# Layer 0's first two modulation vectors from column-tiled float32 matmuls, with their weights in the tiles that later hold h

## The chip, the core and the metric

The kernel runs on one core of a Trainium2 chip. The metric is the device time of one execution in microseconds; a smaller time is better. All numbers ahead of the prediction belong to the kernel before the change.

## What is computed

Two layers of an encoder run over two groups of 512 tokens (g = 0 and 1) with 1024 features. Both groups share all weights; each has its own conditioning vector c. Cut to what matters here:

```python
for l in range(DEPTH):                                     # 2 layers
    mod = (jax.nn.silu(c) @ w_ada[l] + b_ada[l]).reshape(Bsz, 6, 1, D)
    shift_a, scale_a, gate_a = mod[:, 0], mod[:, 1], mod[:, 2]
    shift_f, scale_f, gate_f = mod[:, 3], mod[:, 4], mod[:, 5]
    h = rms_norm(x, norm_attn_g[l]) * (1.0 + scale_a) + shift_a
    proj = h @ w_in[l]
    ...                                                    # four kinds of attention heads
    x = x + gate_a * (mixed @ w_out[l])
    h = rms_norm(x, norm_ffn_g[l]) * (1.0 + scale_f) + shift_f
    x = x + gate_f * conv_glu_ffn(h, ...)
```

Everything is float32. The modulation vectors are numbered c6 = 0 to 5 in the order of the reshape, so c6 = 0 and 1 (shift and scale of the attention norm) are needed before the first h exists, and c6 = 2 to 4 of layer 0 only after the attention.

## The kernel before, in words

Layout: features lie on the 128 partitions in KC = 8 chunks, tokens along the free axis. Large products are made from three matmuls each (`mm3`, lines 172 to 174): both operands are split into a high part (`hh`, `whi`) and a rest (`hl`, `wlo`).

Start of the program (lines 321 to 453, pools `pa`, `pw`, `px`): c is loaded and silu'd into `csx` (line 333). `ada` (line 178) makes a modulation vector from `w_ada`. For c6 = 0 and 1 it is called with `whole=True`, first half (512 columns) of both vectors and then the second half of both: the weights come in pieces of 384 KB on SP's queue (line 191) into seven stage tiles `s` (four of `pw`, three of `pa`), and each piece is multiplied in plain float32, 256 columns at a time, with a stationary operand of 128 x 2 (line 198); 128 such matmuls in all. After each half DVE copies the row out (`arow`, line 205), four small transposes put it on the partitions (line 208), DVE adds the bias (line 216) and, for c6 = 1, makes the gain `ab` (line 225). Between the pieces the hook `interleave` places the eight loads of x (512 KB each, line 354) at the piece numbers `XPOS`. Then come four loads of the first unit's weights (`wt0`, line 379, through `W` of pool `wp`: two stage tiles, a ring of five `whi`/`wlo` pairs; the rest is subtracted by POOL). x is squared and summed (lines 264 to 268), the norm's row is built (lines 274 to 282), and lines 390 to 402 make the 16 pairs `hh`, `hl` from x, the modulation and the norm, mostly on DVE. The pairs live in pool `hp`, 16 tiles of 2 KB for each name.

The last thing in that block (line 453) is `ada(WA, pa, 0, c6, p_tp, p_ov)` for c6 = 2 to 4: 33 more pieces of 384 KB, queued on SP behind the `wt0` loads, each split into `whi` and `wlo` (line 160 on ACT, line 162 on DVE or POOL in the order v, v, p), with three stage tiles and three pairs in `pa`, and `arow` (2 KB, one tile) and `at4` (64 bytes, one tile) for each half vector's end. Its matmuls use the banks `p_tp` and `p_ov`. This is called "the stream" below.

Then the layer loop: nine units (C0, D0, C2, A0, ...) for both g give 18 steps. `project` (line 510) of a step makes four blocks of 128 tokens, 24 matmuls of 384 columns each; ACT copies each block out of its bank to `raw` (line 533) and `V` (line 536). Step 0 (C0, g = 0) uses the banks `p_mm`, `p_mm`, `p_sc`, `p_sc`; later steps of layer 0 use `p_mm` only. There are two banks of `p_mm` and two of `p_sc`. `prepare` (line 569) normalises and transposes `raw` (line 611) and stacks q and k by DMA (line 597). The scores follow (lines 676 and 677), with the bias loaded at line 484, then the softmax's minimum (line 641, writes `S` and `mn`).

Order: the plan at the end of `trunk_kernel` gives a program order, and the framework's list scheduler fixes the order of each engine's instructions when the program is built. Up to eight DMAs of SP's queue are under way at a time (eight semaphores, in turn). 

Memory: the pools lie one behind the other, each tag in the order of its first use, sizes rounded up to 32 bytes. `pa` holds `s` (3 x 3072 bytes per partition), `arow` (2048), `whi` and `wlo` (3 x 3072 each) and `at4` (64): 29,760 bytes. When `pa`, `pw` and `px` are closed, the attention's pools begin at `pa`'s first byte: `ap` (bias, `mx`, `mn`, `den`, `pth`, `ptl` and small tiles: 30,240 bytes), behind it `av` (two `raw` tiles of 4096, three `V` of 4096), then `ar` and `au`. With `reuse_waits="tile"` the first writer of a tile waits until every tile that lay on the same bytes before has been read for the last time. The first `bias` tile has offset 0, as `s`; the first `mn` has offset 9216, as `arow`; step 0's `raw` is the first tile of `av`.

Of the kernel before, what the change touches and what calls it, by code (L numbers as in the profile page):

```python
# [8 lines left out]
F32 = mybir.dt.float32  # L9
# [3 lines left out]
AF = mybir.ActivationFunctionType  # L13
ALU = mybir.AluOpType
# [11 lines left out]
EPS = 1e-6  # L26


P = {'w0': 2.41, 'w1': 2.07, 'b0': 1.49, 'j0': 1.86, 'j1': 1.0, 'p0': 1.06, 'p1': 0.83, 'v': 0.29, 'vd': 0.32, 'f': 0.13, 'fc': 1.16, 'm0': 2.02, 'm1': -0.42, 'o0': 0.58, 'o1': 0.68, 'o2': 0.44, 'a0': 0.66, 'a1': 3.46, 'S': 7, 'K': 6, 'R': 2, 'e': 'p', 'q': 'aa', 'r': 'pv', 'pd': 0.07, 's': -0.28, 'we': 'vvp', 'x': [4, 5, 6, 7, 13, 15, 17, 19], 'hl': 'vpvpvvvv', 'ul': 'v', 'us': 'p', 'ug': 'p', 'uc': 'v', 'uf': 'p', 'tb': 'vpv', 'tl': 'vvvp', 'ds': 'p', 'db': 'p', 'dl': 'vvp', 'd2': 'v', 'ft': [9, 10], 'td': [6, 8], 'fr': [4, 6], 'fs': 3, 'na': 6, 'n1': 2, 'n2': 2, 'gr': [[3, 3, 3], [4, 3, 4]], 'd0': 'v', 'd1': 'v', 't0': 4, 't1': 25, 'sa': [4, 2], 'at': [3.2, 21.2], 'ag': [[4, 4, 0], []]}
UNITS = ['C0', 'D0', 'C2', 'A0', 'D1', 'C1', 'B1', 'A1', 'B0']  # L30
CHUNK = {"A0": 0, "A1": 1, "B0": 2, "B1": 3, "C0": 4, "C1": 5, "C2": 6, "D0": 7, "D1": 8}
GSCALE = {"A": 64 ** -0.5, "B": 64 ** -0.5, "C": 64 ** -0.5, "D": 32 ** -0.5}
# [41 lines left out]
    pass  # L74


def trunk_kernel(tc, xT, cT, w_ada, w_adac, b_ada, norm_g, w_in, w_out, w_out2, w_out9, w_up, w_down, conv, qkn, rpb,
                 amask, t5, onehot, tmask, sink, lam_d, subln, blk, ident_in, out):
    nc = tc.nc
    with ExitStack() as ctx:  # L80
# [94 lines left out]

        ada_last = [None]

        def ada(W, pool, l, c6, bank=None, bank2=None, whole=False, hook=None, halves=(0, 1)):


            acc = None
            R = NG if whole else 2 * NG
            n = W.width // 256
            parts = [(b0, min(n, 16 * halves[-1] + 16 - b0)) for b0 in range(16 * halves[0], 16 * halves[-1] + 16, n)]
            for b0, nb in parts:
                src = w_ada[c6, :, b0 * 256:(b0 + nb) * 256]
                if not whole:
                    w = W.load(src, nb * 256)
                else:
                    w = (W.stage(),)  # L190
                    ada_last[0] = dma(w[0][:, :nb * 256], src).ins
                    hook(ada_last[0])
                for b in range(b0, b0 + nb):
                    half, q, k = b // 16, b // 8 % 2, b % 8
                    if b % 16 == 0:
                        acc = (bank or p_mm)()
                    for j, wj in enumerate(w):
                        nc.tensor.matmul(acc[:R, q * 256:(q + 1) * 256], cs[:, k] if whole else csr[:, k],
                                         wj[:, (b - b0) * 256:(b - b0 + 1) * 256],
                                         start=(k == 0 and j == 0 and q == 0),  # L200
                                         stop=(k == KC - 1 and j == len(w) - 1), skip_group_check=True)
                    if b % 16 < 15:
                        continue
                    row = pool.tile([128, 512], F32, name="arow", bufs=1)
                    nc.vector.tensor_copy(row[:R], acc[:R])
                    pt = (bank2 or p_pp)()
                    for d in range(4):
                        nc.tensor.transpose(pt[:, R * d:R * d + R], row[:R, d * 128:(d + 1) * 128], ident[:R, :R])
                    m = mod[:, l, c6, 4 * half:4 * half + 4]
                    t = pt[:, :4 * R].rearrange("p (a b) -> p a b", b=R)  # L210
                    if not whole:
                        t = pool.tile([128, 4, 4], F32, name="at4", tag="at4", bufs=1)
                        nc.vector.tensor_copy(t.rearrange("p a b -> p (a b)"), pt[:, :16])
                        nc.vector.tensor_tensor(m, t[:, :, 0:2], t[:, :, 2:4], op=ALU.add)
                        t = m
                    nc.vector.tensor_tensor(
                        m, t, bada[:, l, c6 * 8 + 4 * half:c6 * 8 + 4 * half + 4, None].to_broadcast([128, 4, 2]),
                        op=ALU.add)
            ada_gain(l, c6, halves)

        def ada_gain(l, c6, halves=(0, 1)):
            if c6 in (1, 4):
                j = c6 // 3
                a, b = 4 * halves[0], 4 * halves[-1] + 4
                nc.vector.scalar_tensor_tensor(
                    ab[:, l, j, a:b], mod[:, l, c6, a:b], 1.0,
                    ng[:, l, j, a:b, None].to_broadcast([128, b - a, 2]), op0=ALU.add, op1=ALU.mult)
# [93 lines left out]
        with tc.tile_pool(name="pa", bufs=1, reuse_waits="tile") as pa, \  # L321
# [32 lines left out]
                        dma(xs[g][:, k:k + 2], xT[:, g, k:k + 2])  # L354

            WA = Weights(pa, 768, 3, 3, tuple({'p': nc.gpsimd, 'v': nc.vector}[c] for c in P['we']))
            WS = Weights(px, 768, 0, 4)
            WX = Weights(pw, 768, 0, 4)
            stage_of = itertools.cycle((WX, WA, WX, WA, WX, WA, WX))
            WS.stage = lambda: next(stage_of).stage()  # L360
            for c6 in range(2):
                ada(WS, pa, 0, c6, whole=True, hook=interleave, halves=(0,))

            oh = pw.tile([32, 1280], F32, name="oh", bufs=1)
            t5_t = pw.tile([32, 14], F32, name="t5_t", bufs=1)
# [1069 lines left out]
def layout(i):  # L1435

    import numpy as np
    a = {k: np.asarray(v) for k, v in i.items()}
    chunks = lambda v: v.reshape(v.shape[:-1] + (-1, 128))
    r = {}  # L1440
    x = np.stack([a["x_prompt"][0], a["x_sample"][0]])
    r["xT"] = x.transpose(2, 0, 1).reshape(KC, 128, NG, T).transpose(1, 2, 0, 3)
    c = np.stack([a["c_prompt"][0], a["c_sample"][0]])
    r["cT"] = chunks(c).transpose(2, 1, 0)
    r["w_ada"] = a["w_ada"].reshape(DEPTH, KC, 128, 6, 4, 256).transpose(0, 3, 2, 4, 1, 5).reshape(DEPTH, 6, 128, 8192)[0, :5]
    w = a["w_ada"].reshape(DEPTH, KC, 128, 6, D)
# [12 lines left out]
    r["w_out2"] = w[:, others[6:]].transpose(0, 2, 3, 1, 4).reshape(DEPTH, 128, KC * 256)
# [25 lines left out]


# [20 lines left out]
```

## Time and profile before

| what | value |
| --- | --- |
| median of three runs | 2719.42 us (2717.59 to 2723.7) |
| the profiled execution, its own time | 2725.8 us |
| its span in the profile | 2724.0 us |
| TensorE (PE) busy | 2562.2 us, 94% of the span |
| VectorE (DVE) busy | 2018.2 us, 74% |
| ScalarE (ACT) busy | 1410.9 us, 52% |
| GpSimd (POOL) busy | 1143.0 us, 42% |
| granted TensorE clock, mean | 0.976 |

The profile shows one execution. A window row gives, for a stretch of time, each engine's busy time with its count of instructions, the granted TensorE clock, the share of the 16 DMA engines that was busy and the rate. A timeline row gives start, length, engine, line and tiles, with the idle time before it and what ended that. A DMA's row on SP is its issue, not its transfer.

### The profile page before, as it was taken

Reading aid. Unit: us, or ns where it says so; the run is one execution under the profiler, and the core shown is the slowest. Engines: PE = TensorE matmul, PEld = TensorE weight load, DVE = VectorE, ACT = ScalarE, POOL = GpSimd, SP = SyncE. Lnnn points to the kernel's source line nnn. Section 1 sums busy time; section 2 is a strip of 40 time slices with the busy share of each in tenths; the row PEclk is TensorE's granted clock in tenths of the full one; section 3 lists DMA queues with packets and bytes.
Section 4 is the critical chain, followed back from the end, with each engine's and each line's share of the span. In section 5 each row is a group of like instructions: output and inputs, shape, how many; then the busy total and the mean of one; then the engine's idle time right before and its main releaser. Section 6 shows DMA issues by size and latency. Waiting matters only on the chain. (4 is left out here: it accounts for less than half of the span.)

```text
span 2724.0 us, 39807 instructions
## 1 busy us (share of the span) xinstructions
PE 2562.2 (94%) x13836; PEld 2160.4 (79%) x13836; DVE 2018.2 (74%) x3639; ACT 1410.9 (52%) x3058; POOL 1143.0 (42%) x811
## 2 busy tenths in 40 slices
PE   8899999999879999998999999999996999999988
PEld 4788889888657777776788989898875888887767
DVE  6677577665887777789964765867469878878986
ACT  4466566564444445453444756756544555555422
POOL 2321212256644433428853122122667344441884
PEclk9999999999989999999999999999997999999999
DMA  7743545565144444452224345445651222224321
GB/s 265 217 116 107 130 109 141 145 188 181 66 163 144 142 140 128 151 205 101 93 76 113 86 114 136 113 118 148 191 181 47 86 78 87 76 86 185 109 85 62
DMA packets 146433, 347.69 MB, mean 128 GB/s; under 512 B 21372, under 2 KB 27260, under 8 KB 144952
## 3 DMA queue, kind: packets, MB, share of 16 engines
q1 hardware_dynamic: 133560, 322.08, 39.1%
q10 hardware_dynamic: 12672, 23.07, 2.3%
q8 instruction: 109, 1.79, 0.3%
q14 instruction: 92, 0.75, 0.1%
HBM read 241.19 MB, written 59.51 MB: 110 GB/s over the span
## 5 line engine op out<-in xcount | busy, mean ns | idle before, releaser
L162 POOL TENSOR_TENSOR wlo<-s,whi 128x768 fp32r<-128x768 f32 (+1 forms) x131 | 237.3, 1820 | 429.3 <-ACT whi L160 406.2
L172 PE MATMUL ps_mm<-hh,whi 128*128 128x512 f32 x932 | 369.7, 399 | 35.5 <-DVE t L1163 26.2
L173 PE MATMUL ps_mm<-hl,whi 128*128 128x512 f32 x932 | 369.0, 396 | 5.0 <-DVE hl L1094 3.7
L174 PE MATMUL ps_mm<-hh,wlo 128*128 128x512 f32 x932 | 367.5, 394 | 6.3 <-POOL wlo L1094 3.5
L172 PE MATMUL ps_mm<-whi,hh 128*128 128x256 f32 (+1 forms) x1104 | 342.0, 311 | 9.7 <-ACT raw L533 6.7
L173 PE MATMUL ps_mm<-wlo,hh 128*128 128x256 f32 (+1 forms) x1104 | 338.1, 307 | 1.3 <-POOL wlo L162 1.3
L174 PE MATMUL ps_mm<-whi,hl 128*128 128x256 f32 (+1 forms) x1104 | 337.9, 307 | 0.0
L1094 DVE TENSOR_TENSOR wlo<-fr,whi 128x512 fp32r<-128x512 f32 (+1 forms) x385 | 304.0, 807 | 38.2 <-ACT whi L1098 30.3
L1169 POOL TENSOR_TENSOR t<-t 128x512 f32<-128x512 f32 x88 | 127.9, 1453 | 428.0 <-issue 111.3
L1098 ACT ACTIVATE whi<-fr 128x512 fp32r<-128x512 f32 (+1 forms) x416 | 199.6, 517 | 176.3 <-PE ps_mm L173 65.5
L172 PEld LDWEIGHTS ps_mm<-hh,whi 128*128 128x128 f32 x932 | 176.2, 190 | 83.4 <-issue 22.0
L172 PEld LDWEIGHTS ps_mm<-whi,hh 128*128 128x128 f32 x1104 | 214.0, 194 | 13.4 <-ACT raw L533 7.5
L173 PEld LDWEIGHTS ps_mm<-wlo,hh 128*128 128x128 f32 x1104 | 214.3, 194 | 4.2 <-POOL wlo L162 2.2
L174 PEld LDWEIGHTS ps_mm<-whi,hl 128*128 128x128 f32 x1104 | 213.6, 194 | 1.5
L174 PEld LDWEIGHTS ps_mm<-hh,wlo 128*128 128x128 f32 x932 | 176.8, 190 | 44.1 <-POOL wlo L1094 3.9
L173 PEld LDWEIGHTS ps_mm<-hl,whi 128*128 128x128 f32 x932 | 177.0, 190 | 42.5 <-DVE hl L1094 5.4
L160 ACT ACTIVATE whi<-s 128x768 fp32r<-128x768 f32 (+1 forms) x153 | 123.6, 815 | 129.9 <-DMA s<-in_w_in 32.4
L641 DVE CUSTOM_DVE_ANT_0 S<-ps_sc,bias 128x512 f32<-128x512 f32 (+3 forms) x288 | 150.2, 529 | 53.5 <-PE ps_sc L677 41.1
L1161 DVE SCALAR_TENSOR_TENSOR t<-u,cw,t 128x511 f32<-128x511 f32 x120 | 118.1, 984 | 63.4 <-ACT t L1160 62.6
L636 DVE TENSOR_TENSOR ptl<-ps_tp,pth 128x256 fp32r<-128x256 f32 (+1 forms) x240 | 129.7, 552 | 47.8 <-ACT pth L635 46.2
L1160 ACT ACTIVATE t<-u,cw 128x512 f32<-128x512 f32 x120 | 97.6, 813 | 122.8 <-DVE u L1091 107.1
L172 PE MATMUL ps_sc<-hh,whi 128*128 128x512 f32 x404 | 159.1, 395 | 1.1 <-DVE x L1313 1.1
(351 smaller groups left out, 6934.2 us busy)
## 6 DMA issues: line engine op xcount, KB each, us to landing
fr<-in_w_up SPq DMA_DIRECT2D x88, 512.0 KB, 3.8
sa<-in_w_adac SPq DMA_DIRECT2D x56, 512.0 KB, 5.9
s<-in_w_in SPq DMA_DIRECT2D x64, 384.0 KB, 3.6
g_sp<-t ACTq DMA_DIRECT2D x88, 256.0 KB, 4.1
stk<-pr_h SPq DMA_DIRECT2D x152, 128.0 KB, 2.3
stk<-pr_l SPq DMA_DIRECT2D x152, 128.0 KB, 2.4
s<-in_w_ada SPq DMA_DIRECT2D x50, 384.0 KB, 3.3
s<-in_w_out SPq DMA_DIRECT2D x40, 384.0 KB, 3.2
```

The costliest lines, as they stand in the source:

```text
L160: nc.scalar.activation(hi[:, :cols], s[:, :cols], AF.Copy)
L162: self.eng[self.count % len(self.eng)].tensor_tensor(lo[:, :cols], s[:, :cols], hi[:, :cols].bitcast(F32), op=ALU.subtract)
L172: nc.tensor.matmul(out_, a[0], b[0], start=start, stop=False, skip_group_check=True)
L173: nc.tensor.matmul(out_, a[0], b[1], start=False, stop=False, skip_group_check=True)
L174: return nc.tensor.matmul(out_, a[1], b[0], start=False, stop=stop, skip_group_check=True).ins
L636: nc.vector.tensor_tensor(lo[:, :n], pt[:, :n], hi[:, :n].bitcast(F32), op=ALU.subtract)
L641: nc.vector.tensor_tensor_reduce(s[:, :n], p, b, 1.0, init, op0=ALU.add, op1=ALU.min, accum_out=mn)
L1094: pick(key).tensor_tensor(o, a, b, op=ALU.subtract)
L1098: nc.scalar.activation(hi, s, AF.Copy)
L1160: nc.scalar.activation(t, p, AF.Identity, scale=c4[:, 1:2], bias=c4[:, 3:4])
L1161: nc.vector.scalar_tensor_tensor(t[:, 1:], p[:, :T - 1], c4[:, 0:1], t[:, 1:], op0=ALU.mult, op1=ALU.add)
L1169: pick('ug').tensor_tensor(a, a, b, op=ALU.mult)
```

## The change

c6 = 0 and 1 get a function of their own, `ada_half`. Their weights come from a new array `w_adah` in 32 pieces of 256 KB (one chunk of 128 rows by 512 columns each), and the stage tiles are all 32 tiles of `hp`: piece by piece `hh`, `hl`, `hh`, ... so that no piece waits for a tile. Each piece is multiplied by four matmuls of 128 columns with a stationary operand of 128 x 32, each in its own quarter of TensorE's columns (`tile_position`), as `ada_cols` (line 234) does for later vectors with 256 columns. ACT copies the 128 x 128 result to `srow`, a new tag of pool `pa` (512 bytes, two tiles), one full transpose follows, and DVE adds the bias and makes the gain. The four stage tiles of `pw` go, and the stream's `s` tiles are no longer used at the start. `XPOS` is moved to the new piece numbers. `ada` keeps only its split form.

```diff
-P = {... 'x': [4, 5, 6, 7, 13, 15, 17, 19], ...}
+P = {... 'x': [4, 6, 8, 10, 18, 20, 22, 24], ...}
...
-        def ada(W, pool, l, c6, bank=None, bank2=None, whole=False, hook=None, halves=(0, 1)):
+        def ada(W, pool, l, c6, bank, bank2):
...
+        def ada_half(stage, rows, c6, half, hook):
+
+            acc = p_mm()
+            for k in range(KC):
+                s = stage()
+                ada_last[0] = dma(s, w_adah[c6, half, k]).ins
+                hook(ada_last[0])
+                for j in range(4):
+                    nc.tensor.matmul(acc[32 * j:32 * j + 32, :128], csx[:, NG * k:NG * k + 32],
+                                     s[:, j * 128:(j + 1) * 128], start=(k == 0), stop=(k == KC - 1),
+                                     skip_group_check=True, tile_position=(0, 32 * j))
+            row = rows()
+            nc.scalar.activation(row, acc[:, :128], AF.Copy)
+            pt = p_pp()
+            nc.tensor.transpose(pt[:, :128], row, ident)
+            o = c6 * 8 + 4 * half
+            nc.vector.tensor_tensor(mod[:, 0, c6, 4 * half:4 * half + 4],
+                                    pt[:, :128].rearrange("p (j r) -> p j r", j=4)[:, :, :NG],
+                                    bada[:, 0, o:o + 4, None].to_broadcast([128, 4, NG]), op=ALU.add)
+            ada_gain(0, c6, (half,))
...
-            WS = Weights(px, 768, 0, 4)
-            WX = Weights(pw, 768, 0, 4)
-            stage_of = itertools.cycle((WX, WA, WX, WA, WX, WA, WX))
-            WS.stage = lambda: next(stage_of).stage()
+            tags = itertools.cycle(("hh", "hl"))
+
+            def strip():
+                n = next(tags)
+                return hp.tile([128, 512], F32, name=n, tag=n)
+
+            strip_row = lambda: pa.tile([128, 128], F32, name="srow", tag="srow", bufs=2)
             for c6 in range(2):
-                ada(WS, pa, 0, c6, whole=True, hook=interleave, halves=(0,))
+                ada_half(strip, strip_row, c6, 0, interleave)
...
             for c6 in range(2):
-                ada(WS, pa, 0, c6, whole=True, hook=interleave, halves=(1,))
+                ada_half(strip, strip_row, c6, 1, interleave)
```

## Rows read from the trace of the kernel before

**Rows 1.** The page: the busy time and share of each engine.
```profile
PE 2562.2 (94%) x13836; PEld 2160.4 (79%) x13836; DVE 2018.2 (74%) x3639; ACT 1410.9 (52%) x3058; POOL 1143.0 (42%) x811
```

**Rows 2.** Windows: stretch and length, busy PE PEld DVE ACT POOL, clock, DMA share, GB/s.
```profile
4.00:43.40 39.40, 32.85 (x144) 12.00 (x145) 20.48 (x57) 12.89 (x25) 0.00 (x0) 1.00 0.97 347
34.00:36.00 2.00, 2.00 (x11) 0.77 (x10) 1.90 (x5) 0.00 (x0) 0.00 (x0) 1.00 1.04 409
76.00:78.00 2.00, 2.00 (x8) 2.00 (x7) 2.00 (x6) 0.00 (x0) 0.00 (x0) 0.50 0.35 52
47.40:157.00 109.60, 94.13 (x590) 80.60 (x590) 77.87 (x124) 54.63 (x99) 45.18 (x26) 0.97 0.73 203
157.00:200.00 43.00, 40.91 (x263) 37.45 (x264) 34.88 (x97) 32.39 (x90) 8.88 (x5) 0.96 0.39 95
```

**Rows 3.** Timeline of PE, first 50 us: start, length, line, tiles, idle before.
```profile
42.14 4.48 PE L198 MATMUL ps_mm<-s,csx 128*2 128x256 f32 x20
...
47.47 0.42 PE L172 MATMUL ps_mm<-whi,hh 128*128 128x384 f32 x1
```

**Rows 4.** Timeline of SP, 37 to 153 us: start and length of issues, merged.
```profile
37.34 14.39 SPq L167 DMA_DIRECT2D s<-in_w_in  x4
51.83 1.33 SPq L167 DMA_DIRECT2D s<-in_w_ada  x3
...
71.92 18.18 SPq L167 DMA_DIRECT2D s<-in_w_ada  x8
...
150.56 2.12 SPq L484 DMA_DIRECT2D bias<-t5s  x4
```

**Rows 5.** Timeline of DVE, 149 to 158 us: the stream's end, the first softmax.
```profile
149.84 0.69 DVE L162 TENSOR_TENSOR wlo<-s,whi 128x512 fp32r<-128x512 f32 x1
...
152.37 0.68 DVE L205 COPY arow<-ps_tp 4x512 f32<-4x512 f32 x1
...
156.78 0.41 DVE L641 CUSTOM_DVE_ANT_0 S<-ps_sc,bias 128x256 f32<-128x256 f32 x1
```

**Rows 6.** Timeline of PE, 153 to 158 us.
```profile
153.00 0.34 PE L174 MATMUL ps_mm<-whi,hl 128*128 128x384 f32 x1
153.17 0.34 PE L172 MATMUL ps_mm<-whi,hh 128*128 128x384 f32 x1
...
154.33 0.41 PE L208 MATMUL ps_ov<-ident,arow 4*128 4x4 f32 x4
...
157.26 0.58 PE L676 MATMUL ps_sc<-stk 128*128 128x256 f32 x1 [1.93 <-DVE mn L641]
```

**Rows 7.** The tile stk up to 400 us: the scores' weight loads, first and last start.
```profile
L676 PEld LDWEIGHTS ps_sc<-stk x48: 186/190/337, 105.7 to 339.4; 128*128 128x128 f32 x48
```

**Rows 8.** Line 533, 40 to 157 us: ns min/median/max, first and last start.
```profile
L533 ACT ACTIVATE raw<-ps_mm x12: 360/369/391, 66.4 to 154.4; 128x256 f32<-128x256 f32 x12
```

**Rows 9.** PE's groups by line, 47.4 to 157 us: count, busy, mean ns, idle.
```profile
L172 PE MATMUL ps_mm<-whi,hh 128*128 128x384 f32 x96 | 34.1, 357 | 2.9 <-DVE V L537 2.9
...
L198 PE MATMUL ps_tp<-whi,csr 128*4 128x256 f32 x96 | 24.1, 278 | 4.2 <-ACT whi L160 4.1
...
L172 PE MATMUL ps_sc<-whi,hh 128*128 128x384 f32 x16 | 5.0, 335 | 0.0
```

**Rows 10.** The stream's loads and splits, 47.4 to 157 us, by tile and by line.
```profile
L167 SPq DMA_DIRECT2D s<-in_w_ada x33: 327/334/553, 51.8 to 143.4; - x33
DMA to landing us min/median/max: 3.2/3.3/3.3
...
L160 ACT ACTIVATE whi<-s 128x768 fp32r<-128x768 f32 x37 | 30.7, 841 | 36.4 <-DMA s<-in_w_ada 22.7 <-PE ps_tp L198 8.2 <-DVE wlo L162 1.9
L162 DVE TENSOR_TENSOR wlo<-s,whi x22: 690/958/2433, 63.5 to 149.8; 128x768 fp32r<-128x768 f32 x20, 128x512 fp32r<-128x512 f32 x2
L162 POOL TENSOR_TENSOR wlo<-s,whi x20: 1292/1848/2305, 47.8 to 147.8; 128x768 fp32r<-128x768 f32 x19, 128x512 fp32r<-128x512 f32 x1
```

**Rows 11.** Timeline of PE at 761 us: `ada_cols`, one vector's column-tiled matmuls.
```profile
761.12 1.93 PE L242 MATMUL ps_ov<-sa,csx 128*32 128x256 f32 x32
```

More of the change, by code (lines that the diff above doesn't have):

```diff
@@ L26 @@
 EPS = 1e-6
-P = {'w0': 2.41, 'w1': 2.07, 'b0': 1.49, 'j0': 1.86, 'j1': 1.0, 'p0': 1.06, 'p1': 0.83, 'v': 0.29, 'vd': 0.32, 'f': 0.13, 'fc': 1.16, 'm0': 2.02, 'm1': -0.42, 'o0': 0.58, 'o1': 0.68, 'o2': 0.44, 'a0': 0.66, 'a1': 3.46, 'S': 7, 'K': 6, 'R': 2, 'e': 'p', 'q': 'aa', 'r': 'pv', 'pd': 0.07, 's': -0.28, 'we': 'vvp', 'x': [4, 5, 6, 7, 13, 15, 17, 19], 'hl': 'vpvpvvvv', 'ul': 'v', 'us': 'p', 'ug': 'p', 'uc': 'v', 'uf': 'p', 'tb': 'vpv', 'tl': 'vvvp', 'ds': 'p', 'db': 'p', 'dl': 'vvp', 'd2': 'v', 'ft': [9, 10], 'td': [6, 8], 'fr': [4, 6], 'fs': 3, 'na': 6, 'n1': 2, 'n2': 2, 'gr': [[3, 3, 3], [4, 3, 4]], 'd0': 'v', 'd1': 'v', 't0': 4, 't1': 25, 'sa': [4, 2], 'at': [3.2, 21.2], 'ag': [[4, 4, 0], []]}
+P = {'w0': 2.41, 'w1': 2.07, 'b0': 1.49, 'j0': 1.86, 'j1': 1.0, 'p0': 1.06, 'p1': 0.83, 'v': 0.29, 'vd': 0.32, 'f': 0.13, 'fc': 1.16, 'm0': 2.02, 'm1': -0.42, 'o0': 0.58, 'o1': 0.68, 'o2': 0.44, 'a0': 0.66, 'a1': 3.46, 'S': 7, 'K': 6, 'R': 2, 'e': 'p', 'q': 'aa', 'r': 'pv', 'pd': 0.07, 's': -0.28, 'we': 'vvp', 'x': [4, 6, 8, 10, 18, 20, 22, 24], 'hl': 'vpvpvvvv', 'ul': 'v', 'us': 'p', 'ug': 'p', 'uc': 'v', 'uf': 'p', 'tb': 'vpv', 'tl': 'vvvp', 'ds': 'p', 'db': 'p', 'dl': 'vvp', 'd2': 'v', 'ft': [9, 10], 'td': [6, 8], 'fr': [4, 6], 'fs': 3, 'na': 6, 'n1': 2, 'n2': 2, 'gr': [[3, 3, 3], [4, 3, 4]], 'd0': 'v', 'd1': 'v', 't0': 4, 't1': 25, 'sa': [4, 2], 'at': [3.2, 21.2], 'ag': [[4, 4, 0], []]}
 UNITS = ['C0', 'D0', 'C2', 'A0', 'D1', 'C1', 'B1', 'A1', 'B0']
@@ L74, with trunk_kernel @@
     pass
-def trunk_kernel(tc, xT, cT, w_ada, w_adac, b_ada, norm_g, w_in, w_out, w_out2, w_out9, w_up, w_down, conv, qkn, rpb,
+def trunk_kernel(tc, xT, cT, w_ada, w_adah, w_adac, b_ada, norm_g, w_in, w_out, w_out2, w_out9, w_up, w_down, conv, qkn, rpb,
                  amask, t5, onehot, tmask, sink, lam_d, subln, blk, ident_in, out):
@@ L176, in trunk_kernel @@
         ada_last = [None]
-        def ada(W, pool, l, c6, bank=None, bank2=None, whole=False, hook=None, halves=(0, 1)):
+        def ada(W, pool, l, c6, bank, bank2):
             acc = None
-            R = NG if whole else 2 * NG
+            R = 2 * NG
             n = W.width // 256
[L184 to L192, printed above, removed]
+            for b0 in range(0, 32, n):
+                nb = min(n, 32 - b0)
+                w = W.load(w_ada[c6 - 2, :, b0 * 256:(b0 + nb) * 256], nb * 256)
                 for b in range(b0, b0 + nb):
@@ L195, in ada @@
                     if b % 16 == 0:
-                        acc = (bank or p_mm)()
+                        acc = bank()
                     for j, wj in enumerate(w):
-                        nc.tensor.matmul(acc[:R, q * 256:(q + 1) * 256], cs[:, k] if whole else csr[:, k],
+                        nc.tensor.matmul(acc[:R, q * 256:(q + 1) * 256], csr[:, k],
                                          wj[:, (b - b0) * 256:(b - b0 + 1) * 256],
@@ L205, in ada @@
                     nc.vector.tensor_copy(row[:R], acc[:R])
-                    pt = (bank2 or p_pp)()
+                    pt = bank2()
                     for d in range(4):
@@ L209, in ada @@
                     m = mod[:, l, c6, 4 * half:4 * half + 4]
[L210 to L215, printed above, removed]
+                    t = pool.tile([128, 4, 4], F32, name="at4", tag="at4", bufs=1)
+                    nc.vector.tensor_copy(t.rearrange("p a b -> p (a b)"), pt[:, :16])
+                    nc.vector.tensor_tensor(m, t[:, :, 0:2], t[:, :, 2:4], op=ALU.add)
                     nc.vector.tensor_tensor(
-                        m, t, bada[:, l, c6 * 8 + 4 * half:c6 * 8 + 4 * half + 4, None].to_broadcast([128, 4, 2]),
+                        m, m, bada[:, l, c6 * 8 + 4 * half:c6 * 8 + 4 * half + 4, None].to_broadcast([128, 4, 2]),
                         op=ALU.add)
-            ada_gain(l, c6, halves)
+            ada_gain(l, c6)
+        def ada_half(stage, rows, c6, half, hook):
[17 more added lines that the diff above has]
+            ada_gain(0, c6, (half,))
         def ada_gain(l, c6, halves=(0, 1)):
@@ L1444, in layout @@
     r["cT"] = chunks(c).transpose(2, 1, 0)
-    r["w_ada"] = a["w_ada"].reshape(DEPTH, KC, 128, 6, 4, 256).transpose(0, 3, 2, 4, 1, 5).reshape(DEPTH, 6, 128, 8192)[0, :5]
+    r["w_ada"] = a["w_ada"].reshape(DEPTH, KC, 128, 6, 4, 256).transpose(0, 3, 2, 4, 1, 5).reshape(DEPTH, 6, 128, 8192)[0, 2:5]
     w = a["w_ada"].reshape(DEPTH, KC, 128, 6, D)
+    r["w_adah"] = w[0, :, :, :2].reshape(KC, 128, 2, 2, 512).transpose(2, 3, 0, 1, 4)
     r["w_adac"] = np.stack([w[l, :, :, c6].reshape(KC, 128, D) for l, c6 in ADAT])
@@ L1480, in layout @@
     return {k: np.ascontiguousarray(v) for k, v in r.items()}
-ARGS = ["xT", "cT", "w_ada", "w_adac", "b_ada", "norm_g", "w_in", "w_out", "w_out2", "w_out9", "w_up", "w_down", "conv", "qkn",
+ARGS = ["xT", "cT", "w_ada", "w_adah", "w_adac", "b_ada", "norm_g", "w_in", "w_out", "w_out2", "w_out9", "w_up", "w_down", "conv", "qkn",
         "rpb", "amask", "t5", "onehot", "tmask", "sink", "lam_d", "subln", "blk", "ident_in"]
```

## The prediction

> **What bounds the kernel now.** The page comes first: PE is busy for 94% of the span [rows 1], so over most of the program a microsecond in which PE has nothing to do is a microsecond of time, and work on another engine is free while PE is fed. The windows then show where PE isn't fed. In the first 43 us the DMA engines are busy for 0.97 of the time at 347 GB/s, and reach 409 GB/s in the best stretches [rows 2]: that stage is bound by its 8.4 MB of modulation weights and 4.2 MB of x. From 47.4 to 157 us PE is busy for 94.1 of 109.6 us and the clock has dips [rows 2]; this is the stage to read closely, since its end is set by something else than PE.
>
> That end can be read from three rows. The first scores are loaded at 105.7 us [rows 7], but the first softmax starts only at 156.78 [rows 5], and PE then goes on at 157.26, after 1.93 us of idleness [rows 6]. What came late is memory, not data: the bias loads are issued at 150.56 [rows 4], and the last reader of a stream tile `s`, the `wlo` of 149.84 + 0.69, ended at 150.53 [rows 5]. The bias tile lies where `s` lay. `mn` lies where `arow` lay, and the last `arow` was copied at 152.37 [rows 5] and read by PE until 154.33 + 0.41 = 154.74 [rows 6]. So the attention can't begin before the stream for c6 = 2 to 4 has ended, and PE fills the wait with projections. It can, because step 0's `raw` is free: ACT writes it from 66.4 us on [rows 8], 90 us before the stream's end.
>
> **The change part by part.**
>
> *The loads.* 24 pieces that had to wait for seven tiles become 32 that wait for none, of the same 8.4 MB. From 4 to 43.4 us at 347 GB/s 13.7 MB moved [rows 2], 0.8 MB of it the first two `wt0` pieces, so 12.9 MB go ahead of them. At 347 GB/s they take 37 us, at 409 GB/s 32 us [rows 2]; no row shows 2 KB rows in eight pieces at a time alone, so these are the ends, and I take 34.5, with the last piece at 38.5 instead of about 41. The Trainium skill would have it otherwise: "DMA: Bandwidth & Descriptors", Specifications, gives one core 358 GB/s of HBM, by which an estimate of the last piece is 40 us; the trace's 409 GB/s disagrees.
>
> *The matmuls.* Before, 128 matmuls; the last 20 ran from 42.14 to 46.62, a backlog behind data that was there, and the first real matmul started at 47.47 [rows 3]. Column-tiled, 32 matmuls of 256 columns take 1.93 us [rows 11], so 128 of 128 columns cost between 128 / 32 x 1.93 / 2 = 3.9 us (cost by columns) and 7.7 us (cost by instruction), or twice that at half clock. All but the last piece's lie beside transfers; the tail after the last piece (four matmuls, a copy, a transpose, two DVE steps) is about 2 us. The backlog is gone: `h` of the second half and the first `wt0` pieces are there at about 41 us, 6.5 us earlier.
>
> *The stream's start.* `wt0` pieces 3 and 4 wait for `W`'s two stage tiles, so for POOL's `wlo` of 1.85 us each [rows 10]. Before, the four took until 51.8, where the stream's first issue is [rows 4]: 8 us after the loads of c6 = 0 and 1. Kept at 7.5 us, the stream starts at 46, 5.8 us earlier. If nothing else changed, this would be the gain.
>
> *The memory of `raw`.* `pa` gets the tag `srow`, 2 x 512 = 1024 bytes, and it is the first one used. Then `s`, `whi`, `wlo` take 27,648 bytes; `arow` lies at 28,672 to 30,720 and `at4` at 30,720 to 30,784. Before, `pa` ended at 29,760, and `av` begins at 30,240, behind `ap`, which the change leaves alone. So step 0's `raw` now lies on the last 480 bytes of `arow` and on `at4`, and by the rule that held back `bias` and `mn` [rows 4 to 6] ACT can't copy step 0's blocks out before the stream has ended. Queued behind this: ACT's copies of step 0; its four banks, which are both `p_mm` and both `p_sc`; so every projection of step 1 and later, and all scores. PE keeps 96 of the projection matmuls (step 0) and the stream's own 192, in `p_tp` and `p_ov`. The stream itself isn't blocked, so nothing hangs.
>
> *When the stream ends.* A stage tile's turn: landing 3.3 us, `whi` 0.84, `wlo` 0.96 on DVE or 1.85 on POOL [rows 10], and some 0.3 us of handing over: 5.4 or 6.3 us. With three tiles, one of which always goes to POOL, three pieces take 6.3 us: 2.1 us each. Before, eight issues in a row took 18.18 us, so 2.5 us each [rows 4], with DVE full (2.00 of 2.00 us at 76 us [rows 2]) and PE's queue in the way; all 33 issues took 51.8 to 143.4 [rows 10]. After the change DVE, ACT and PE have little else to do from about 60 us on. From 46 us, 32 x 2.1 = 67 us: last issue at 113; its landing, splits, matmuls, `arow`, transposes and `at4` take 7 us (3.3 + 0.7 + 0.7 + 0.7 + 0.7 + 0.4 and handing over): 120 us. Ends: 1.95 us a piece gives 115, 2.5 gives 133.
>
> *The sum.* Until 157 us PE had done 96 + 16 = 112 projection matmuls of each of the three kinds [rows 9], 336 in all, 3.5 steps. After the change 96 are done when the stream ends, and 240 are left, at 0.173 us (153.00 to 153.17 [rows 6]): 41.6 us, with 3 us of transposes and scores 45. PE restarts on them after a long lean stretch: at 76 to 78 us, after little work, the granted clock was 0.50, the lower level (1.2 GHz) [rows 2], so I add 2 us; the copy out of the banks 0.7 us; and PE's idle share right after, 5% (40.91 of 43 us busy [rows 2]), 2.3 us. 120 + 50 = 170 us, where before 157.3 us stood. I take 1 us off for attention that is ready sooner by then: +12 us. Behind it PE bounds as before, and the loss stays. The profiled execution took 2725.8 us, its span 2724.0, 6.4 us (0.2%) above the median; the difference is put on the median: 2719.4 + 12 = 2731.4 us.
>
> **The rivals.**
>
> *The wait doesn't bind* (step 0's `raw` gets bytes that are free, because the tags lie otherwise than I count, or because the second `raw` tile is taken). Then the front's gain of 5.8 to 6.5 us counts, and DVE, ahead by some 10 us, also fills the gaps near 70 us (the 2.9 us wait for `V` [rows 9] and the half clock after it): -8 us, 2711.4 us. For it: nothing in the change asks for `raw`. Against it: the byte counts, and `bias` issued 0.03 us after the last read of `s`. It ends on the other side.
>
> *The wait binds, but is paid for.* The stream alone on DMA, DVE and ACT ends at 110 (1.85 us a piece from 46), or step 1 rather than step 0 gets the blocked `raw`, so PE loses half as much. The point from which the change loses is a stream's end near 108 us: 108 + 50 = 158. It gives 0 to +5 us: 2722.
>
> *A slower stream.* The scheduler puts `w_in` loads of D0, which can't be split while step 0 and 1 hold the ring, ahead of stream pieces on SP, or DVE stays full for longer: 2.5 us a piece, end at 133, +25 us, 2744. Against it: SP issued stream pieces between other loads before.
>
> *Not what it says*: that the column tiles don't overlap. Then 128 matmuls cost at most what they did, and lie beside transfers; below 2 us, inside the others.
>
> **How the numbers follow.** The forecast (wait binds, stream ends at 114 to 126) has 0.52; the slower stream 0.13; paid for 0.20; no wait 0.15. What a measurement of this kernel can tell from no change is about 0.2%, 5.4 us. Forecast: 0.45 of its 0.52 lies above +5.4, 0.07 within; slower stream all; paid for all within; no wait 0.12 faster, 0.03 within. So slower 0.45 + 0.13 = 0.58, same 0.07 + 0.20 + 0.03 = 0.30, faster 0.12. The range: from -8 us, where half of the first rival is still in, to +25 us: 2711 to 2745. The forecast's own range is 2726 to 2738.
>
> **What would show it.** Right: `raw` of step 0 written only behind the last `arow` and `at4`; from about 60 us PE with the stream's matmuls alone; 33 stream issues from 46 to about 113 us; projections of step 1 behind them; the granted clock low in between. The front would show in modulation done near 41 us and no idle SP. Wrong: `raw` written near 60 us, or a stream's end below 108 us or above 130. A first softmax much before 157 us with a longer time would say that the loss is elsewhere.

## The result, and the profile after

The changed kernel takes 2743.31 us (median of 6 runs, 2739.46 to 2748.96) where the kernel before took 2718.32 beside it: ratio 1.0091, 95% interval 1.0075 to 1.0106, so 24.7 us slower. That is inside the predicted range of 2711 to 2745 us, twice the predicted difference of 12 us, and above the forecast's own range of 2726 to 2738; the wider range held it because it took in the rival of a slower stream. All differences below are ratios to the kernel before of the same chip, put on 2718.3 us, since the kernel before took up to 2724 us beside later runs.

The changed kernel's profiled execution took 2745.99 us, its span 2744.2. Its windows, in the columns of [rows 2] (stretch and length, busy PE, PEld, DVE, ACT, POOL, clock, DMA share, GB/s):

```profile
4.00:43.40 39.40, 26.96 (x281) 11.29 (x281) 20.50 (x39) 15.15 (x29) 2.60 (x2) 0.99 0.95 350
34.00:36.00 2.00, 1.91 (x32) 0.94 (x32) 2.00 (x5) 1.58 (x3) 0.00 (x0) 1.00 1.06 407
47.40:157.00 109.60, 82.58 (x453) 62.50 (x453) 66.25 (x129) 48.45 (x80) 36.94 (x22) 0.80 0.56 165
```

Up to 43 us the DMA engines move what they moved before. The loss is in the next stretch: PE busy for 82.6 us instead of 94.1, and at a granted clock of 0.80 instead of 0.97, so even the busy time holds less work: 453 matmul records against 590.

What PE lacked is shown by ACT. Its timeline around 125 us (start, length, engine, line, tiles, in brackets the idle time before and what ended it):

```profile
123.93 1.36 ACT L160 ACTIVATE whi<-s 128x768 fp32r<-128x768 f32 x2 [3.04 <-DMA s<-in_w_ada]
129.79 0.38 ACT L547 ACTIVATE raw<-ps_mm 128x256 f32<-128x256 f32 x1 [4.50 <-DVE mod L205]
```

This is the first write of `raw` (line 533 before, 547 now). Before it came at 66.4 us [rows 8]; now ACT sits idle for 4.5 us with step 0's banks full, until DVE's line 205 has ended. DVE's timeline has that instruction, the last reader of `at4`:

```profile
129.53 0.17 DVE L205 TENSOR_TENSOR mod<-at 128x8 f32<-128x8 f32 x1
```

It ends at 129.70, and `raw` starts 0.09 us later. The stream's end is thus E = 129.7 to 129.8 us, where the prediction had 120. SP's queue, merged as in [rows 4], shows how the stream got there:

```profile
48.58 1.37 SPq L167 DMA_DIRECT2D s<-in_w_ada  x3
...
55.43 3.88 SPq L167 DMA_DIRECT2D s<-in_w_in  x2
60.79 3.68 SPq L167 DMA_DIRECT2D s<-in_w_ada  x3
65.85 0.33 SPq L167 DMA_DIRECT2D s<-in_w_in  x1
68.17 53.59 SPq L167 DMA_DIRECT2D s<-in_w_ada  x27
```

Six pieces are issued up to 68.17, with loads of `w_in` for step 2 between them; then 27 follow without another load between. Their mean distance is 2.05 us, but they don't come evenly. The same rows asked for from 73 to 78 us and from 79 us on, then DVE's row at 72.63:

```profile
73.60 3.27 SPq L167 DMA_DIRECT2D s<-in_w_ada  x3
79.37 42.39 SPq L167 DMA_DIRECT2D s<-in_w_ada  x23
```

```profile
72.63 0.95 DVE L162 TENSOR_TENSOR wlo<-s,whi 128x768 fp32r<-128x768 f32 x1
```

The eighth piece is issued at 73.60, 5.4 us behind the seventh: its stage tile came free when this `wlo` ended at 73.58, and the `wlo` had stood in DVE's queue behind `hh` and `hl` of g = 1. From the eleventh piece (79.37) to the last (121.43) the distance is 1.91 us. What PE had done by 157.3 us, from 40 us on, in the columns of [rows 9]:

```profile
L191 PE MATMUL ps_tp<-wlo,csr 128*4 128x256 f32 x96 | 31.1, 346 | 20.3 <-POOL wlo L162 11.8 <-DVE wlo L162 8.5
...
L172 PE MATMUL ps_mm<-whi,hh 128*128 128x384 f32 x60 | 21.7, 371 | 1.4 <-DVE V L551 1.4
...
L172 PE MATMUL ps_sc<-whi,hh 128*128 128x384 f32 x16 | 5.6, 360 | 0.0
```

Of each of the three kinds of projection matmul 60 + 16 = 76 are done, where before 96 + 16 = 112 were [rows 9]. 36 x 3 = 108 are missing; at 0.173 us [rows 6] that is 18.7 us. The first softmax starts as early as before (156.78 in [rows 5]); here is its row in the changed kernel:

```profile
156.24 0.42 DVE L655 CUSTOM_DVE_ANT_0 S<-ps_sc,bias 128x256 f32<-128x256 f32 x1 [2.00 <-PE ps_sc L691]
```

So the attention isn't late, the projections are. The first scores of a wide unit tell what it costs by then; the first fence below is the tile `stk` of the kernel before, the second of the changed kernel (ns min/median/max, first and last start within 90 to 220 us):

```profile
L732 PE MATMUL ps_sc<-stk x20: 392/396/481, 176.8 to 218.8; 96*128 96x512 f32 x20
```

```profile
L746 PE MATMUL ps_sc<-stk x10: 394/401/503, 205.5 to 218.2; 96*128 96x512 f32 x10
```

28.7 us are lost there, and a part is won back later: at the end the two profiled executions differ by 20.2 us.

### The profile page after: what moved, and what is told of

Same layout as the page of the kernel before. It is cut to its first block, busy times and chain, and to the rows that moved or that the text cites. A ratio compares the mean times of both kernels' runs of the same rounds, so it can differ in the third digit from the quotient of the medians.

```text
span 2744.2 us, 40054 instructions
## 1 busy us (share of the span) xinstructions
PE 2565.3 (93%) x13952; PEld 2164.8 (79%) x13952; DVE 2016.1 (73%) x3635; ACT 1414.1 (52%) x3062; POOL 1139.1 (42%) x811
## 4 chain that ended last, share of the span: by engine, by line
PE 37%; DVE 6%; issue 3%; DMA 2%; POOL 1%; ACT 1%; SPq 1%; POOLq 0%; DVEq 0%; ACTq 0%
PE ps_mm L172 7%; PE ps_mm L173 7%; PE ps_mm L174 7%; PE ps_sc L172 2%; PE ps_sc L173 2%; PE ps_sc L174 2%; PE ps_tp L174 2%; PE ps_tp L173 2%; PE ps_tp L172 2%; DVE wlo L1108 1%; DMA s<-in_w_in 1%; DVE x L1327 1%; DVE hl L1108 1%; PE ps_sc L690 0%; SPq L611 0%
## 5 line engine op out<-in xcount | busy, mean ns | idle before, releaser
L1108 DVE TENSOR_TENSOR wlo<-fr,whi 128x512 fp32r<-128x512 f32 (+1 forms) x385 | 307.8, 817 | 36.7 <-ACT whi L1112 28.8
L172 PEld LDWEIGHTS ps_mm<-whi,hh 128*128 128x128 f32 x1104 | 214.4, 195 | 14.2 <-ACT raw L547 7.0
```

The lines of the kernel that those rows point to most:

```text
L172: nc.tensor.matmul(out_, a[0], b[0], start=start, stop=False, skip_group_check=True)
L1108: pick(key).tensor_tensor(o, a, b, op=ALU.subtract)
```

## The experiments

Theory: the 25 us are the wait of `raw` for memory that the stream holds. Rival: they lie in the new front, in its column-tiled matmuls, its small pieces, the meeting of DVE and POOL and the low clock. Line numbers are those of the changed kernel; the two runs made from the kernel before have its own.

### srow in another pool

```diff
-            strip_row = lambda: pa.tile([128, 128], F32, name="srow", tag="srow", bufs=2)
+            strip_row = lambda: pw.tile([128, 128], F32, name="srow", tag="srow", bufs=2)
```

> The changed kernel with srow in pool pw instead of pa, so that pa is 29,760 bytes again and step 0's raw no longer lies on arow and at4. Theory of the wait: ACT writes the first raw near 64 us (129.79 in the changed kernel), PE fills the stream's time with step 1's projections, and the time falls below the kernel before by what the front gained: first real matmul 2.9 us earlier, so 2710 to 2716 us. Rival, the cost lies in the new front (column-tiled matmuls, pieces of 256 KB, DVE beside POOL, the low clock at the start): raw early, yet the time stays at 2735 to 2745.

Measured: ratio 0.9978 (0.9969 to 0.9986), 6.0 us faster than the kernel before and 30.7 faster than the changed one, by moving 1024 bytes. The front is the same to 0.4 us (first real matmul at 44.91 and 44.54 us). Its tile `raw`, then PE's groups from 40 to 157.3 us, then its tile `stk`:

```profile
L547 ACT ACTIVATE raw<-ps_mm x12: 365/384/387, 75.8 to 150.3; 128x256 f32<-128x256 f32 x12
```

```profile
L172 PE MATMUL ps_mm<-whi,hh 128*128 128x384 f32 x96 | 34.2, 360 | 0.5 <-ACT whi L160 0.4
...
L172 PE MATMUL ps_sc<-whi,hh 128*128 128x384 f32 x16 | 5.6, 360 | 0.0
```

```profile
L746 PE MATMUL ps_sc<-stk x22: 392/396/495, 173.0 to 219.9; 96*128 96x512 f32 x22
```

112 of each kind again, and the wide unit's scores 3.8 us earlier than before. The rival falls. `raw` came at 75.8 and not near 64: in ACT's queue a split of the stream stood ahead of it and waited from 69.17 to 75.03, so some of PE's idleness near 70 us stays.

### The wait alone, in the kernel before

```diff
-            nc.vector.memset(csx, 0.0)
+            nc.vector.memset(csx, 0.0); nc.vector.memset(pa.tile([128, 128], F32, name="pad", bufs=1), 0.0)
```

`pad` is never used again; the second run has `[128, 120]`, so 480 bytes instead of 512.

> The kernel before with one unused tile of 512 bytes placed first in pa, nothing of the change: pa is 30,272 bytes, 32 more than the offset at which raw begins, so step 0's raw shares 32 bytes with at4. Theory of the wait: the first raw is written only when the last at4 has been read; the stream, which starts at 51.8 instead of 48.6 us, ends near 133; 2740 to 2750 us. Rival (cost in the new front): 2718 plus or minus 4.

> As the run with 512 bytes, but 480 bytes: pa ends at 30,240, exactly where raw begins, so no byte is shared. Theory of the wait: 2718 plus or minus 4, the first raw at 66 us as before. Any theory by which a larger pa, the extra first instruction, or the shifted pools behind it cost time: as with 512 bytes.

Measured: with 512 bytes 1.0102 (1.0085 to 1.0119), 27.7 us slower; with 480 bytes 1.0002 (0.9992 to 1.0012), no difference. ACT's and DVE's timelines with 512 bytes, then ACT's with 480:

```profile
134.25 0.38 ACT L533 ACTIVATE raw<-ps_mm 128x256 f32<-128x256 f32 x1 [5.30 <-DVE mod L214]
```

```profile
134.05 0.17 DVE L214 TENSOR_TENSOR mod<-at 128x8 f32<-128x8 f32 x1
```

```profile
66.96 0.36 ACT L533 ACTIVATE raw<-ps_mm 128x256 f32<-128x256 f32 x1
```

With 480 bytes `pa` ends at 30,240, where `av` begins; with 512 its last 32 bytes, a part of `at4`, lie under `raw`, and the copy starts 0.03 us behind the last reader of `at4`. 32 bytes per partition cost 27 us; a larger pool as such costs nothing.

### The stream's pace

```diff
-P = {... 'we': 'vvp', ...}
+P = {... 'we': 'v', ...}
```

> The changed kernel with all 33 rests wlo of the stream on DVE (0.96 us each) instead of every third on POOL (1.85 us). Theory of the wait: the time follows the stream's end about one to one; a tile's turn falls from 6.3 to 5.4 us, three tiles, so 1.8 instead of 2.05 us for each of the later 27 pieces, 7 us in all, less some 1 to 3 us because DVE is full until 77 us: stream's end 123 to 126, time 2737 to 2740 us. Rival (cost in the new front): 2743 plus or minus 3.

Measured: 1.0096 (1.0081 to 1.0111), 26.1 us slower than before, 1.4 more than the changed kernel and not 3 to 6 less. SP's, POOL's and DVE's timelines:

```profile
62.39 3.73 SPq L167 DMA_DIRECT2D s<-in_w_ada  x3
76.56 0.33 SPq L167 DMA_DIRECT2D s<-in_w_in  x1
77.02 6.20 SPq L167 DMA_DIRECT2D s<-in_w_ada  x4
84.35 40.83 SPq L167 DMA_DIRECT2D s<-in_w_ada  x23
```

```profile
64.31 12.23 POOL L162 TENSOR_TENSOR wlo<-s,whi 128x768 fp32r<-128x768 f32 x1 [4.46 <-ACT whi L160]
```

```profile
73.90 0.96 DVE L162 TENSOR_TENSOR wlo<-s,whi 128x768 fp32r<-128x768 f32 x1
```

The last 27 pieces began at 77.02, 8.9 us later (0.9 us of it from the stream's first issue on). Their pace was near the expected 1.8: from the eleventh piece (84.35) to the last 1.84 us each. But the expected gain of 7 us was reckoned from 2.05, which holds the 5.4 us stop; over the same pieces the changed kernel's pace was 1.91, so taking the rests off POOL was worth 1.6 us there, and the eleventh piece came 5.0 us later. One POOL subtraction, for a piece of `w_in`, took 12.23 us instead of 1.85 [rows 10]. DVE worked without a gap until 73.90 + 0.96 = 74.86, and POOL's ended 1.68 us behind that. SP's next `w_in` issue needed that stage tile, and the stream's pieces stood behind it. So E went to 132.0 (the first `raw`), up by 2.2 us, and the time by 1.4, which the two intervals can't tell from nothing: the expectation's number missed, the link between E and the time isn't contradicted, and the step is too small to settle the slope.

### A larger step of the stream's end

In `ada`, the same edit in the changed kernel and in the one with `srow` in `pw` (`W.s` is the stage tile of the last load). It leaves out 21 of the stream's 33 loads and makes c6 = 3 and 4 from other weights, so it is a probe of the wait and no version to keep:

```diff
-                w = W.load(w_ada[c6 - 2, :, b0 * 256:(b0 + nb) * 256], nb * 256)
+                w = W.load(w_ada[c6 - 2, :, b0 * 256:(b0 + nb) * 256], nb * 256) if c6 < 3 or (c6, b0) == (3, 0) else W.split(W.s, nb * 256)
```

> The changed kernel, in which 21 of the stream's 33 pieces are not loaded: from the first piece of c6 = 3 on every split is made from that piece's tile. Modulation c6 = 3 and 4 is thus computed from other weights, splits and matmuls stay all. The stream then goes at the pace of splits and matmuls, 1.0 to 1.4 us a piece instead of 2.05, and ends at 108 to 115 us instead of 129.8. Theory of the wait, one to one as in the prediction's sum (break-even at a stream's end of 108 us): 2718 to 2728 us. Rival, the wait costs only a part of each microsecond, since PE has the stream's own matmuls to do meanwhile (31 us between the changed kernel and the one with srow elsewhere, over some 58 us from the end of step 0's matmuls to the stream's end, so 0.5 us per us): 2731 to 2736.

> The run with srow in another pool, with the same 21 loads left out. Its stream, which shares PE with projections, ends 15 to 25 us earlier, and bias and mn with it. If the stream's end still sets the start of the attention and PE's gaps there: 2708 to 2714 us. If PE was full enough with projections that the gate hardly mattered: 2714 to 2718. Against the changed kernel with fewer loads it gives the price of the wait for raw with a stream's end near 110: 5 us or less one to one, some 18 us by parts.

Measured: in the changed kernel 1.0042 (1.0029 to 1.0055), 11.4 us slower than before; with `srow` elsewhere 0.9958 (0.9942 to 0.9974), 11.4 us faster. ACT's timeline of the first, and the row of its first softmax:

```profile
114.81 0.38 ACT L547 ACTIVATE raw<-ps_mm 128x256 f32<-128x256 f32 x1 [4.32 <-DVE mod L205]
```

```profile
142.05 0.42 DVE L655 CUSTOM_DVE_ANT_0 S<-ps_sc,bias 128x256 f32<-128x256 f32 x1 [2.16 <-PE ps_sc L691]
```

| kernel | first `raw`, us | time against before, us (95% interval) |
| --- | --- | --- |
| changed, fewer loads | 114.8 | +11.4 (7.9 to 15.0) |
| changed | 129.8 | +24.7 (20.4 to 28.8) |
| changed, stream on DVE | 132.0 | +26.1 (22.0 to 30.2) |
| before, 512 bytes | 134.3 | +27.7 (23.1 to 32.3) |

From the first two, 13.3 us for 15.0 us of E: 0.9 us per us, near the prediction's one to one; the half of the rival would have given 8. The intervals allow some 8 to 19 us for that difference, so the times alone don't exclude the half. The traces, one execution each, speak for one to one: the first softmax starts 14.2 us earlier (156.24 to 142.05). Carried on at this slope, the loss is zero near E = 102 us (114.8 - 11.4 / 0.89), an extrapolation; the prediction put that point at 108. The time, 2718.3 + 11.4 = 2729.7 us, lies between the two expected ranges (2718 to 2728, and 2731 to 2736 for the rival).

The price of the wait by itself, against the kernel with the same loads and `srow` elsewhere, is 30.7 us at E = 129.8 and 22.8 at 114.8, so 0.53 us per us. Both can hold: the other 5.4 us are gained without the wait too. With `srow` elsewhere the stream shares PE with the projections and its end moved much less than the 15 to 25 us expected: the last read of `at4` from 150.98 to 146.93 us, and the first softmax with it from 152.61 to 148.56, 4.05 us each, which fits a stream that ends earlier and so frees `mn` earlier.

### What the front could still give

The second norm behind the first group's pairs in the program order, with `srow` in `pw` (`hs = []` stands ahead of the loop then, and the loop over the pairs follows inside it):

```diff
             for g in range(NG):
                 acc = px.tile([128, T], F32, name="n_acc", tag="n_acc", bufs=2)
                 for k in range(KC):
                     square(pft, acc, xs[g][:, k], k == 0)
                 pbs.append(norm_scale(acc))
-            hs = []
-            for g in range(NG):
                 hs.append([])
```

> As the run with srow in another pool, and the sum of squares of g = 1 with its norm's row stands behind the pairs of g = 0 in the program order, so that on PE the last transpose of srow comes ahead of the matmuls of that sum, for which PE waited 2.81 us in the changed kernel. If the rest of the front's forecast gain (first real matmul 2.9 us earlier instead of 6.5) was lost in this order: first real matmul at 41 to 42 us instead of 44.5, and 2711 to 2716 us, 2 to 4 us below the run with srow elsewhere. If the end of that stage is set by the stream's end (bias and mn lie where s and arow lay) and not by the front: no change, 2717 plus or minus 3; or a loss, when g = 1 comes later.

Measured: 1.0027 (1.0015 to 1.0038), 7.3 us slower than before, 13 more than without the edit. PE's timeline near 42 us, and DVE's near 75:

```profile
40.90 0.33 PE L225 MATMUL ps_pp<-ident,srow 128*128 128x128 f32 x1 [0.40 <-ACT srow L223]
42.27 0.62 PE L172 MATMUL ps_mm<-whi,hh 128*128 128x384 f32 x2 [1.04 <-ACT whi L160]
...
46.48 0.69 PE L173 MATMUL ps_mm<-wlo,hh 128*128 128x384 f32 x1 [3.24 <-POOL wlo L162]
```

```profile
74.50 5.35 DVE L412 SCALAR_TENSOR_TENSOR n_t<-x,ab,ps_tp 128x512 f32<-128x512 f32 x8 [7.67 <-PE ps_tp L293]
```

The transpose came 3.9 us earlier (44.80 to 40.90) and the first real matmul at 42.27; then PE waited 3.24 us for POOL's first `wlo`, and g = 1, whose norm waited for PE's queue, began at 74.5. The last of the three expectations, a loss because g = 1 comes later.

The stream's rests on DVE, with `srow` in `pw`:

> The run with srow in another pool, with all rests of the stream on DVE. In the changed kernel this gave 1.78 us a piece but a loss of 9 us at one POOL instruction of 12.23 us while DVE worked without a gap. If the same happens: 2717 to 2722 us. If DVE has gaps there: the stream ends some 5 us earlier and 2713 to 2717 us.

Measured: 1.0018 (1.0007 to 1.0028), 4.9 us slower than before, a little above the 2717 to 2722 us expected for this case. The same POOL instruction has the same length, 12.22 us from 64.18 on.

The `hl` of g = 0 on DVE alone (`'hl': 'vvvvvvvv'`), then also the rests of the first eight `w_in` pieces, with the stream's rests on DVE (POOL kept free) or still in the order v, v, p:

> The run with srow in another pool, and the two of every four rests hl of g = 0 that POOL made are made by DVE too. In that run POOL made two of them from 40.75 to 44.05 us and only then the first wlo of the first unit's weights (to 46.3), while DVE needed 3.97 us for two hl of 0.69 each. If this meeting of POOL and DVE is what took the rest of the front's forecast gain: the first wlo is done near 43 us, projections flow 2 to 4 us earlier, and 2713 to 2717 us against 2717.8 (ratio to the kernel before 0.9960 to 0.9975 against 0.9978). If DVE, busy for 9.96 of 10 us there, is the bound by itself, four hl more cost it 2.8 us: ratio 0.9980 to 0.9995.

> srow in another pool, and from 40 to 77 us POOL gets no work: the hl of g = 0, the rests of the first eight pieces of w_in and all rests of the stream are made by DVE. Reading so far: a POOL subtraction (1.8 to 2.3 us) and a DVE operation with two tiles hold each other up, one of 12.23 us and hl of 2.3 and 2.4 us instead of 0.69 among them. If so, one engine alone gets through sooner: 11 rests of 0.95 us and 2 hl of 0.69 more on DVE are 12 us, against 20 us that POOL was busy from 40 to 70 us; no DVE operation of its kind above 1.1 us; the first wlo done near 42.5 us; 2708 to 2715 us (ratio 0.994 to 0.997). If the two only share the work, DVE is the longer queue: step 0 and its raw 8 to 12 us later, 2718 to 2728 us.

> As the run with POOL kept free, but every third rest of the stream stays on POOL. If the two engines hold each other up, the few POOL subtractions of 60 to 77 us still cost DVE or the stream some us, while behind 80 us POOL takes a third of the stream's rests off DVE, which is free there anyway: within 4 us of that run, on either side, 2709 to 2718 us.

Measured: 0.9976 (0.9964 to 0.9987), 0.9994 (0.9981 to 1.0006) and 1.0014 (1.0002 to 1.0026): 6.5 us faster than before, which the 6.0 without the edit can't be told from, then 1.6 faster (no difference), then 3.8 slower. DVE's timeline and the tile `stk` with POOL kept free:

```profile
41.93 2.49 DVE L416 TENSOR_TENSOR hl<-n_t,hh 128x512 fp32r<-128x512 f32 x4
44.34 0.95 DVE L162 TENSOR_TENSOR wlo<-s,whi 128x768 fp32r<-128x768 f32 x1
```

```profile
L746 PE MATMUL ps_sc<-stk x25: 392/396/481, 167.5 to 219.4; 96*128 96x512 f32 x25
```

Four `hl` take 2.49 us, where two took 3.97 beside POOL, and the wide unit's scores 5.5 us earlier than with `srow` elsewhere alone. Yet the time isn't lower: the first split of the layer's second half (line 1108) starts at 684.3 us in this kernel and at 684.7 in the other, so the lead was gone by then. Which of the changed orders between 220 and 680 us gave it back wasn't traced, and stays open. POOL and DVE in the last of the three:

```profile
67.85 6.21 POOL L162 TENSOR_TENSOR wlo<-s,whi 128x768 fp32r<-128x768 f32 x1 [10.09 <-ACT whi L160]
```

```profile
71.72 0.67 DVE L416 TENSOR_TENSOR hl<-n_t,hh 128x512 fp32r<-128x512 f32 x1
```

A single POOL subtraction left in DVE's unbroken row of work takes 6.21 us, ends 1.67 us after it, and moves the stream's seventh piece from 67.95 (POOL kept free) to 74.08. The expected gains (1 to 5 us for the first, 3 to 10 for the second) didn't come, and the third was 5.4 us slower than the second, where 4 us on either side was expected.

The version that beats both kernels by the smallest edit is the changed one with `srow` in `pw`.

## Why the prediction came out as it did

*The cause was right.* `raw` on `arow` and `at4`, found from the byte counts, is the whole loss: without it the change gains 6.0 us, and without the change it costs 27.7. "The wait doesn't bind" was priced at 8 us of gain; the run with `srow` elsewhere gave 6.0.

*The mis-sized term is the stream's end.* 120 us forecast, 129.7 measured; at 0.9 us per us these 9.7 us of E are 8.6 us of the 12.7 that the forecast was short. By parts of its own sum (rounded, the parts come to 9.6):

- The start, 46 us forecast, 48.58 measured: +2.6.
- The first ten steps, to the eleventh piece, 2.1 us each or 21.0: measured 48.58 to 79.37, 30.8: +9.8. This is the step that failed. "DVE, ACT and PE have little else to do from about 60 us on" was true from 77 us on. SP's longer stops ended with POOL subtractions at 55.41, 58.95, 60.77, 65.83 and 68.14 us and with DVE's at 64.12 and 73.58. Those at 55.41, 58.95 and 65.83 held back `w_in` pieces, whose stage tiles POOL frees and which stand in the same queue ahead of the stream's; the others held the stream's own stage tiles. The same block could be read before: there the seventh piece, the first of the eight in a row, was issued 71.92 - 51.83 = 20.1 us behind the first [rows 4]. The sum counted a pace from the first piece on.
- The next 22, 2.1 us each or 46.2: measured 42.1, 1.91 each, -4.1. The turn of a stage tile, worked out from durations, was 10% too long. That the 26 steps behind the seventh piece average 2.05 is two errors that cancel, this one and the stop of 5.4 us.
- The tail, 7 us forecast: last issue 121.4, last read 129.70: +1.3.

The rival "a slower stream" named the right cause (loads of `w_in` ahead of the pieces, DVE full for longer) and gave E = 133 and 2744 us, the nearest time of all, but by a pace of 2.5 us a piece that wasn't there: the delay was one block at the start, so the near hit is luck. It got 0.13 against 0.52 for a stream in which nothing is in the way; that weight was wrong, since nothing in the rows of before showed an unhindered stream before 72 us. A slip beside it: by its own terms "paid for" ends its stream at 46 + 32 x 1.85 + 7 = 112 us, not 110.

*The front gave less than its 6.5 us.* The loads were right: the last piece was there at 39.49 us (forecast 38.5, before about 41). The Trainium skill, "DMA: Bandwidth & Descriptors", Specifications, gives 358 GB/s as one core's limit, its half of a stack's 716; the 407 GB/s at 34 to 36 us is again above it. The pieces' matmuls kept to their price: where they ran back to back a piece took 0.24 us (36.75 to 36.99) to 0.43 us (33.91 to 34.34), so 7.7 to 13.8 us for 32, where 3.9 to twice 7.7 was put down. The tail behind the last piece, 2 us forecast, wasn't. PE's timeline of the changed kernel, then POOL's:

```profile
39.49 0.43 PE L219 MATMUL ps_mm<-hl,csx 128*32 128x128 f32 x8 [0.21 <-DMA hl<-in_w_adah]
42.73 1.84 PE L285 MATMUL ps_tp<-ones,n_acc 128*128 128x1 f32 x8 [2.81 <-DVE n_acc L279]
44.44 0.45 PE L225 MATMUL ps_pp<-ident,srow 128*128 128x128 f32 x1
44.54 0.99 PE L172 MATMUL ps_mm<-whi,hh 128*128 128x384 f32 x2
```

```profile
42.12 1.59 POOL L416 TENSOR_TENSOR hl<-n_t,hh 128x512 fp32r<-128x512 f32 x1 [0.42 <-issue]
43.68 4.50 POOL L162 TENSOR_TENSOR wlo<-s,whi 128x768 fp32r<-128x768 f32 x2
```

In PE's queue the second group's sum stood ahead of the last transpose and waited 2.81 us for DVE, and the first `wlo` stood behind `hl` on POOL. The first real matmul came 2.9 us earlier than before (44.54, 47.47 in [rows 3]) instead of 6.5. The prediction costed the tail as a chain of its own and didn't ask what stood beside it in each queue. That the rest of the 6.5 us could be had by another order isn't shown: of the five runs that moved work between queues and engines none was measurably faster than `srow` elsewhere.

*The 50 us behind the stream's end* weren't taken up as put down: PE didn't first do all 240 projections and then the scores; the softmax began at 156.24 with 108 missing. With the measured E the sum gives 129.8 + 50 - 157.3 - 1 = 21.5 us, against 24.7; that it comes so near by an order of work that didn't happen is in part luck.

## What to carry to other kernels

When a change adds bytes to a pool, work out which tile of the next pools begins there and when the last of the bytes beneath it is read; 32 bytes cost 27.7 us here, and `srow`'s 1024 bytes in a pool that is free early cost nothing. Size a wait by the time at which its last reader ends, and take that reader's pace from the stretch in which it will run, with the loads that share its queue, not from its unhindered turn. A new tile can be harmless itself and still push a long-lived neighbour: with `srow` in `pw` step 0's `raw` lies, by the layout of the pools, on `srow`, last read near 45 us, and nothing waits; with `srow` in `pa` it lay on `arow` and `at4`.

## What the runs showed of the hardware

POOL and DVE held each other up much further than the 1.85 and 0.96 us of [rows 10] tell. A POOL subtraction with two inputs took 12.23, 12.22 and 6.21 us where DVE had work without a gap, and ended 1.68 and 1.67 us after DVE's last operation in the two cases worked out above, about its own length alone; that it waited until then, and didn't run slowly, is inferred from these ends. The other way round, DVE's `hl` of 0.68 us took 2.32 at 66.37 us of the changed kernel, beside a POOL subtraction of 1.87 at 66.27. The Trainium skill, "SBUF — State Buffer", "SBUF: two separate sides", has a rule for it: the two engines share a pair of ports as a lock that one instruction holds to its end, so that the other one waits; of DVE's instructions this goes for those with two inputs in SBUF or in a mode that uses two ports. The traces fit it, and if this lock is what held POOL, it need not change hands between DVE's instructions: eighteen of them ran during the one wait of 12.23 us. It isn't always so: the changed kernel's subtraction at 63.41 us took 2.42 us, though DVE was busy for all of 60 to 68 us.

Starved of work, PE also lost its clock. Windows of the changed kernel, of the one with `srow` elsewhere, and one of the kernel before:

```profile
70.00:110.00 40.00, 23.57 (x131) 11.84 (x132) 24.32 (x36) 15.54 (x19) 10.29 (x6) 0.71 0.58 178
110.00:130.00 20.00, 12.60 (x67) 6.61 (x65) 9.78 (x17) 6.64 (x9) 5.42 (x3) 0.67 0.52 170
```

```profile
70.00:110.00 40.00, 35.63 (x230) 29.88 (x231) 26.89 (x48) 21.91 (x42) 13.79 (x8) 0.91 0.71 207
110.00:130.00 20.00, 17.51 (x96) 13.79 (x95) 11.38 (x22) 8.33 (x17) 8.85 (x5) 0.83 0.84 241
```

```profile
110.00:130.00 20.00, 17.27 (x118) 14.16 (x117) 15.07 (x25) 10.41 (x19) 9.43 (x5) 1.00 0.92 262
```

Busy for 36.2 of the 60 us, PE was granted 0.71 and 0.67 of its clock on average, a mixture of the two levels (2.4 and 1.2 GHz); busy for 53.1, it was granted 0.91 and 0.83. The busy share alone doesn't set it: from 110 to 130 us the kernel before was busy for no more than the one with `srow` elsewhere, and was granted 1.00. The stream's matmuls took 346 ns on average instead of 278 [rows 9].
